# Setup's two transposes side by side, one more step between decay and outputs of the state space, and the row of its inverse norms put off by two units

## The chip, the core and the metric

The kernel runs on one core of one Trainium2 chip. A core has five engines with a queue each: TensorE (PE) for matrix products, VectorE (DVE), ScalarE (ACT), GpSimd (POOL), and SyncE (SP), which here only starts transfers. Each engine works through its own queue in order; an instruction that waits for another engine holds up what is queued behind it. The metric is the time of one execution in microseconds (us). Before the change it is 1207.95, the median of three runs (1207.37 to 1208.33).

## What is computed

Two layers over 256 tokens with 1024 features. Each layer adds to a residual `h` a gated feed-forward part, a mixer, and another feed-forward part. The mixer has a state-space branch of 16 heads in 2 groups, and an attention branch in which each token sees the 64 keys that an index score picks.

```python
for i in range(DEPTH):                                       # DEPTH = 2
    h = h + 0.5 * swiglu_ffn(rmsnorm(h, norm_ffn1[i]), w_ffn1_in[i], w_ffn1_out[i])
    u = rmsnorm(h, norm_mix[i]) @ w_mix_in[i]
    z, xbc, dt_raw, q, k, v, q_idx, k_idx, w_idx = jnp.split(u, SPLIT_POINTS, axis=-1)
    y_ssd = ssd_mixer(z, xbc, dt_raw, conv_w[i], conv_b[i], dt_bias[i], a_log[i], d_skip[i], ssd_norm[i])
    y_att = dsa_mixer(q, k, v, q_idx, k_idx, w_idx, positions)
    h = h + jnp.concatenate([y_ssd, y_att], axis=-1) @ w_mix_out[i]
    h = h + 0.5 * swiglu_ffn(rmsnorm(h, norm_ffn2[i]), w_ffn2_in[i], w_ffn2_out[i])
return rmsnorm(h, final_norm)
# the state space, per head: causal products with a decay exp(cs[l] - cs[s])
#   y = einsum('gls,gels,gsep->glep', C B^T, decay, x * dt) + x * d_skip
#   y = y * silu(z);  per group of 512 features: y * rsqrt(mean(y*y) + eps) * norm_g
```

## The kernel before

Every large product is made of three: an operand is split into a high and a low part, and PE forms high x high, high x low and low x high (`three`, L186 to L188; the mixer's channels L915 to L917). I call these main matmuls. They write 512 columns into one of the PSUM banks of the pools `mm` and `ac`, two banks each; short products and transposes use the pools `sd` and `tp`, two banks each. A bank can be written again only when it has been read.

Weights come through SP's queue in blocks of 128 x 2048 into a ring of three raw tiles. ACT casts each to its high part (`whi`, L128), DVE subtracts that from the raw tile (`wlo`, L129). These pairs are a ring of three as well: the cast of a new block waits until PE has done the last matmul of the block whose tiles it takes (`Stream.done`).

Side work is cut into generators, which `Flow.step` takes in turn, one step each time, between pieces of the main work; a `yield` ends a step. `Flow.defer(fn, units)` puts a function off by some units, and `Flow.unit` marks the end of one (in the output product 12 main matmuls). A scheduler then sets the final order on each engine from that program.

The mixer first projects in the order of `MIX_ORDER`, with the state space (`ssd`, added to the side work after channel 6) between q, k and v. For each group of 8 heads `ssd` fetches the running sums of the decay for 4 heads at a time into one of the two buffers of the ring `six()` (a transfer that POOL starts, L756), lets ACT form the decay (L758 to L763), lets DVE multiply it by C B^T (L764, L765), and lets PE form the outputs (L774, L778). `finish_y` then gates them, squares them, sums the squares on PE (`sums`, L805), takes the power -1/2 on POOL (L809), spreads the result over a bank by PE (`row`, L815), and scales and splits the outputs into `yT` (L824 to L827). The product with the output weights (`out_product`) goes through `yT` in pairs of 128-feature channels and calls `need` for each: 0 to 3 belong to the first group, 4 to 7 to the second, 8 to 15 to attention. Where one is missing, side work is stepped until it is there. Attention runs beside it: scores (L849), mask and maximum on DVE (L852, L856), exponentials on ACT (L859), division on DVE (L862, L863), transposes (L881 to L883) and outputs of each head (L871, L873), which ACT and DVE split (L876, L877).

Setup transposes two small tables on PE, gains (L377) and convolution weights (L379), into two places of one bank, and DVE copies each out (L378, L380).

Of the kernel before, what the change touches and what calls it, by code (L numbers as in the profile page):

```python
# [52 lines left out]
def hybrid_kernel(  # L53
# [6 lines left out]
    nc = tc.nc  # L60
# [288 lines left out]
    def setup():  # L349

        def later(*a, **k):
            tc.keep_in_program_order(nc.sync.dma_start(*a, **k))

        with tc.tile_pool(name="setup", bufs=1, reuse_waits="tile") as tmp:
            rows = tmp.tile([64, P], F32, name="rows")
            for i, v in enumerate((norm_ffn1, norm_mix, norm_ffn2, ssd_norm)):
                later(rows[16 * i:16 * i + 16, :], v.rearrange("l (k p) -> (l k) p", p=P))
            yield
            crows = tmp.tile([120, P], F32, name="crows")
            later(crows[0:96, :], conv_w.rearrange("l j (c p) -> (l j c) p", p=P))  # L360
            later(crows[96:120, :], conv_b.rearrange("l (c p) -> (l c) p", p=P))
            yield
            pos_i = tmp.tile([P, NT], I32, name="pos_i")
            later(pos_i, positions.rearrange("o (t p) -> p (o t)", p=P), allow_slow_non_contiguous=True)
            frq = tmp.tile([P, NF], F32, name="frq")
            later(frq, inv_freq.partition_broadcast(P))
            yield
            for i, v in enumerate((dt_bias, a_log, d_skip)):
                later(heads[:, i], v.partition_broadcast(P))
            yield  # L370
            for _ in range(3):
                yield
            for i in range(2):
                nc.gpsimd.tensor_copy(skips[64 * i:64 * i + 64],
                                      heads[64 * i:64 * i + 64, 2].rearrange("p l (c i) -> p l c i", i=2)[..., i])
            pg = bank(sd)
            nc.tensor.transpose(pg[:, 0:64], rows, ident[:64, :64])  # L377
            nc.vector.tensor_copy(gains, pg[:, 0:64])  # L378
            nc.tensor.transpose(pg[:, 128:248], crows, ident[:120, :120])  # L379
            nc.vector.tensor_copy(convs, pg[:, 128:248])  # L380
            yield
            pos = tmp.tile([P, NT], F32, name="pos")
            nc.vector.tensor_copy(pos, pos_i)
            ang = tmp.tile([P, NT, NF], F32, name="ang")
            turn = tmp.tile([P, NT, NF], F32, name="turn")
            for t in range(NT):
                nc.vector.tensor_scalar(ang[:, t], frq, pos[:, t:t + 1], None, op0=ALU.mult)
            yield
            RND = 12582912.0
            for period in (TWO_PI * 2048.0, TWO_PI):  # L390
                nc.vector.tensor_scalar(turn, ang, 1.0 / period, None, op0=ALU.mult)
                nc.vector.tensor_scalar(turn, turn, RND, None, op0=ALU.add)
                nc.vector.tensor_scalar(turn, turn, -RND, None, op0=ALU.add)
                for part in _pieces12(period, 3):
                    nc.vector.scalar_tensor_tensor(ang, turn, -part, ang, op0=ALU.mult, op1=ALU.add)
                yield
            PI_IN = 3.1415925
            nc.vector.tensor_scalar(ang, ang, PI_IN, -PI_IN, op0=ALU.min, op1=ALU.max)
            quarter = tmp.tile([P, NT, NF], F32, name="quarter")
            nc.vector.scalar_tensor_tensor(quarter, ang, -1.0, ang, op0=ALU.mult, op1=ALU.min)  # L400
            nc.vector.tensor_scalar(quarter, quarter, TWO_PI / 4, None, op0=ALU.add)
            yield
            cos_f = tmp.tile([P, NT, NF], F32, name="cos_f")
            sin_f = tmp.tile([P, NT, NF], F32, name="sin_f")
            nc.scalar.activation(cos_f, quarter, AF.Sin)
            nc.scalar.activation(sin_f, ang, AF.Sin)
            yield
            for name, c0 in (("att", 0), ("idx", 16)):
                cc, ss, n = ropes[name]
                for t in range(NT):  # L410
                    for half in range(2):
                        nc.gpsimd.tensor_copy(cc[:, t, half * n:(half + 1) * n], cos_f[:, t, c0:c0 + n])
                    nc.vector.tensor_scalar(ss[:, t, 0:n], sin_f[:, t, c0:c0 + n], -1.0, None, op0=ALU.mult)
                    nc.gpsimd.tensor_copy(ss[:, t, n:2 * n], sin_f[:, t, c0:c0 + n])
            yield
# [155 lines left out]
    def mixer(l, norm, after):  # L571
        with ExitStack() as mctx:
# [165 lines left out]
            def ssd():  # L738
                cb = ms.tile([P, G_SSD, 384], F32, name="cb")
                for g in range(G_SSD):  # L740
                    ps = bank(sd)
                    bm, cm = chan[8 + g], chan[10 + g]
                    nc.tensor.matmul(ps[:, 0:L], bm[:, 0:P], cm, start=True, stop=True)
                    nc.tensor.matmul(ps[:, L:L + P], bm[:, P:L], cm[:, P:L], start=True, stop=True)
                    nc.vector.tensor_mul(cb[:, g, 0:L], ps[:, 0:L], mask01)
                    nc.vector.tensor_mul(cb[:, g, L:384], ps[:, L:384], triu)
                yield
                for g in range(G_SSD):
                    ms4 = []
                    for h0 in (0, 4):  # L750
                        m = six()
                        m0 = m[:, 0:1024].rearrange("p (h c) -> p h c", h=4)
                        m1 = m[:, 1024:1536].rearrange("p (h c) -> p h c", h=4)
                        ms4.append((m0, m1))
                        hh = 8 * g + h0
                        nc.gpsimd.dma_start(m0, csum[hh:hh + 4, :].partition_broadcast(P))  # L756
                        for h in range(4):
                            nc.scalar.activation(m1[:, h], m0[:, h, P:], AF.Relu, scale=-1.0,  # L758
                                                 bias=cs[:, 1, hh + h:hh + h + 1])
                            nc.scalar.activation(m0[:, h], m0[:, h], AF.Relu, scale=-1.0,  # L760
                                                 bias=cs[:, 0, hh + h:hh + h + 1])
                        nc.scalar.activation(m0, m0, AF.Exp, scale=-1.0)
                        nc.scalar.activation(m1, m1, AF.Exp, scale=-1.0)  # L763
                        nc.vector.tensor_mul(m0, m0, bc(cb[:, g, 0:L], [P, 4, L], 1))  # L764
                        nc.vector.tensor_mul(m1, m1, bc(cb[:, g, L:384], [P, 4, P], 1))  # L765
                        yield
                    half = xs[:, :, 512 * g:512 * g + 512]
                    pss = [bank(ac) for _ in range(2)]
                    for h in range(0, 8, 2):
                        o = pss[h // 4][:, h % 4 * P:h % 4 * P + L]  # L770
                        m0, m1 = ms4[h // 4]
                        for j in range(2):
                            tc.keep_in_program_order(
                                nc.tensor.matmul(o[64 * j:64 * j + 64], half[:, 0, (h + j) * 64:(h + j + 1) * 64],  # L774
                                                 m0[:, (h + j) % 4], start=True, stop=False))
                        for j in range(2):
                            tc.keep_in_program_order(
                                nc.tensor.matmul(o[64 * j:64 * j + 64, P:], half[:, 1, (h + j) * 64:(h + j + 1) * 64],  # L778
                                                 m1[:, (h + j) % 4], start=False, stop=True))
                    finish_y(g, half, pss)  # L780
                    yield

            def finish_y(g, half, pss):
# [18 lines left out]
                def sums():  # L802
                    ps = bank(sd)
                    for t in range(NT):
                        nc.tensor.matmul(ps[:, t:t + 1], sz[:, 4 * g, t * P:(t + 1) * P], ones[:, 0:1],  # L805
                                         start=True, stop=True)
                    m, rg = (small.tile([P, NT], F32, name=n) for n in ("ms_y", "r_y"))
                    nc.vector.tensor_scalar(m, ps[:, 0:NT], 2.0 / D_SSD, EPS, op0=ALU.mult, op1=ALU.add)
                    nc.gpsimd.tensor_tensor(rg, m, mhalf.to_broadcast([P, NT]), ALU.pow)  # L809
                    flow.defer(lambda: row(rg))  # L810

                def row(rg):
                    rT = bank(sd)[:, :L]
# [223 lines left out]
```

## Time and profile before

| what | value |
|---|---|
| median of 3 runs | 1207.95 us |
| profiled execution | 1208.47 us |
| its span, first to last instruction | 1206.8 us |
| PE busy | 1192.7 us, 99% |
| DVE busy | 738.4 us, 61% |
| ACT busy | 634.1 us, 53% |
| POOL busy | 101.9 us, 8% |
| moved by DMA | 214.26 MB, 178 GB/s over the span |

The profiled execution is the one that all times of the trace come from; 1.67 us of it lie outside the span. The share of PE says that the kernel is as long as PE's work and waits; the list of PE's waits is short. The other engines' shares are averages over parts with different work. In the rows a tile's name stands without its number, and "x4" behind a row are several like instructions in one.

### The profile page before, as it was taken

What the parts mean: (1) busy time and instruction counts of PE and PEld (TensorE: products, weight loads), DVE (VectorE), ACT (ScalarE), POOL (GpSimd) and SP (SyncE); (2) the same over time, 40 slices, a digit from 0 to 9 for tenths busy, and PEclk for the clock granted to TensorE, in tenths of its full rate; (3) what the DMA queues carried; (4) which work ended last, traced back from release to release, by engine and by line L of the source; (5) the groups of instructions that cost most, each with busy time, mean ns of one, the idle gap of its engine ahead of it and who ended that gap; (6) DMA issues with size and microseconds to landing.
All of it is one profiled execution on the core that took longest, in us unless ns stands there. A gap on an engine that the chain in (4) does not pass through costs nothing.

```text
span 1206.8 us, 15519 instructions
## 1 busy us (share of the span) xinstructions
PE 1192.7 (99%) x6125; PEld 1002.6 (83%) x6125; DVE 738.4 (61%) x948; ACT 634.1 (53%) x847; POOL 101.9 (8%) x206
## 2 busy tenths in 40 slices
PE   9999999999999999999999999999999999999997
PEld 7788888998777888888888888899987788888886
DVE  5645545796797555544465554467868965554544
ACT  7544435658775544443354444366478555444432
POOL 1200000502410000000000000014133000000000
PEclk9999999999999999999999999999999999999999
DMA  9565555654534465555655645466455435556550
GB/s 291 171 205 184 186 175 165 210 175 158 192 140 145 135 210 187 164 207 188 196 161 188 201 163 198 163 205 196 145 191 192 140 122 174 191 164 204 183 200 36
DMA packets 152909, 214.26 MB, mean 178 GB/s; under 512 B 8068, under 2 KB 123012, under 8 KB 152836
## 3 DMA queue, kind: packets, MB, share of 16 engines
q1 hardware_dynamic: 151108, 207.99, 52.6%
q0 software_dynamic: 1280, 4.23, 1.0%
q8 instruction: 48, 0.79, 0.3%
q10 hardware_dynamic: 448, 1.05, 0.2%
q14 instruction: 25, 0.20, 0.1%
HBM read 212.17 MB, written 1.08 MB: 177 GB/s over the span
## 4 chain that ended last, share of the span: by engine, by line
PE 89%; ACT 5%; DMA 2%; DVE 1%; issue 1%; POOL 1%; SPq 0%; POOLq 0%; ACTq 0%
PE mm L187 14%; PE mm L188 13%; PE mm L186 13%; PE ac L188 11%; PE ac L187 11%; PE ac L186 11%; PE mm L915 2%; PE ac L915 2%; PE mm L917 2%; PE ac L916 2%; PE ac L917 2%; PE mm L916 2%; PE tp L541 2%; ACT whi L128 1%; PE sd L849 1%
## 5 line engine op out<-in xcount | busy, mean ns | idle before, releaser
L129 DVE TENSOR_TENSOR wlo<-raw,whi 128x2048 fp32r<-128x2048 f32 (+3 forms) x208 | 451.7, 2176 | 325.2 <-ACT whi L128 324.4
L128 ACT CAST whi<-raw 128x2048 fp32r<-128x2048 f32 (+3 forms) x208 | 376.8, 1818 | 285.5 <-PE ac L188 193.0
L186 PE MATMUL mm<-whi,tT 128*128 128x512 f32 (+1 forms) x640 | 255.2, 399 | 0.0
L187 PE MATMUL mm<-wlo,tT 128*128 128x512 f32 (+1 forms) x640 | 247.9, 387 | 0.9 <-DVE wlo L129 0.9
L188 PE MATMUL mm<-whi,tT 128*128 128x512 f32 (+1 forms) x640 | 248.1, 388 | 0.0
L186 PE MATMUL ac<-whi,tT 128*128 128x512 f32 (+1 forms) x448 | 176.5, 394 | 0.0
L188 PE MATMUL ac<-whi,tT 128*128 128x512 f32 (+1 forms) x448 | 173.3, 387 | 0.0
L187 PE MATMUL ac<-wlo,tT 128*128 128x512 f32 (+1 forms) x448 | 173.1, 386 | 0.0
L187 PEld LDWEIGHTS mm<-wlo,tT 128*128 128x128 f32 x640 | 120.6, 188 | 24.1 <-DVE wlo L129 1.4
L188 PEld LDWEIGHTS mm<-whi,tT 128*128 128x128 f32 x640 | 120.3, 188 | 24.4
L186 PEld LDWEIGHTS mm<-whi,tT 128*128 128x128 f32 x640 | 120.6, 188 | 23.5 <-issue 1.3
L188 PEld LDWEIGHTS ac<-whi,tT 128*128 128x128 f32 x448 | 84.3, 188 | 16.4
L187 PEld LDWEIGHTS ac<-wlo,tT 128*128 128x128 f32 x448 | 84.6, 189 | 15.4 <-DVE wlo L129 0.4
L186 PEld LDWEIGHTS ac<-whi,tT 128*128 128x128 f32 x448 | 84.3, 188 | 14.7
L186 PE MATMUL ac<-whi,hT_hi 128*128 128x512 f32 x176 | 69.3, 394 | 0.0
L186 PE MATMUL mm<-whi,hT_hi 128*128 128x512 f32 x176 | 69.0, 392 | 0.0
L188 PE MATMUL ac<-whi,hT_lo 128*128 128x512 f32 x176 | 68.6, 390 | 0.0
L188 PE MATMUL mm<-whi,hT_lo 128*128 128x512 f32 x176 | 68.6, 390 | 0.0
L187 PE MATMUL mm<-wlo,hT_hi 128*128 128x512 f32 x176 | 68.5, 389 | 0.0
L187 PE MATMUL ac<-wlo,hT_hi 128*128 128x512 f32 x176 | 68.5, 389 | 0.0
L450 POOL TENSOR_TENSOR r_x<-ms_x,mhalf 128x1 f32<-128x1 f32 x12 | 6.6, 547 | 670.7 <-DVE ms_x L448 663.2
L563 ACT ACTIVATE s1k<-mm,r_x 128x256 f32<-128x256 f32 x44 | 20.7, 471 | 69.7 <-PE mm L188 69.7
(230 smaller groups left out, 1604.6 us busy)
## 6 DMA issues: line engine op xcount, KB each, us to landing
raw<-in_w_ffn_in_dram SPq DMA_DIRECT2D x172, 512.0 KB, 4.9
raw<-in_w_ffn_out_dram SPq DMA_DIRECT2D x44, 1024.0 KB, 4.9
raw<-in_w_mix_in_dram SPq DMA_DIRECT2D x44, 1024.0 KB, 5.2
raw<-in_w_mix_out_dram SPq DMA_DIRECT2D x16, 1024.0 KB, 4.8
s<-csum POOLq DMA_DIRECT2D x8, 512.0 KB, 4.1
raw<-in_w_mix_in_dram SPq DMA_DIRECT2D x4, 600.0 KB, 3.9
raw<-in_w_mix_in_dram SPq DMA_DIRECT2D x4, 568.0 KB, 3.9
raw<-in_w_ffn_in_dram SPq DMA_DIRECT2D x8, 256.0 KB, 6.0
```

Source lines behind the costliest of these rows:

```text
L128: pin(nc.scalar.copy(hi[:, o], raw[:, o]))
L129: pin(nc.vector.tensor_sub(lo[:, o], raw[:, o], hi[:, o].bitcast(F32)))
L186: nc.tensor.matmul(ps, xh, whi, start=first, stop=False)
L187: nc.tensor.matmul(ps, xh, wlo, start=False, stop=False)
L188: nc.tensor.matmul(ps, xl, whi, start=False, stop=last)
L450: nc.gpsimd.tensor_tensor(r, m, mhalf, ALU.pow)
L541: nc.tensor.transpose(ps[:, f * L + t * P:f * L + (t + 1) * P], hs[:, t, f * P:(f + 1) * P], ident)
L563: nc.scalar.activation(sg, ps[:, 0:256], AF.Silu, scale=norm.r[t])
L849: nc.tensor.matmul(ps[:, j * nk:(j + 1) * nk], qT[:, hg + h0 + j, t * P:(t + 1) * P], kT[:, hg + h0 + j, 0:nk], start=True, stop=True)
L915: nc.tensor.matmul(ps, hi[:, o:o + P], xh, start=(k == 0), stop=False)
L916: nc.tensor.matmul(ps, hi[:, o:o + P], xl, start=False, stop=False)
L917: nc.tensor.matmul(ps, lo[:, o:o + P], xh, start=False, stop=(k == KD - 1))
```

## The change

Three edits. In setup both transposes are issued before the first copy. In `ssd` one more `yield` stands between the last decay of a group and its outputs, so another generator or a piece of main work can come between. The function `row` is put off by two units and not by one. Behind the added line every line number is one higher: L774 is L775, L815 is L816, L877 is L878, L882 is L883.

```diff
--- before.py
+++ after.py
@@ -375,8 +375,8 @@
                                       heads[64 * i:64 * i + 64, 2].rearrange("p l (c i) -> p l c i", i=2)[..., i])
             pg = bank(sd)
             nc.tensor.transpose(pg[:, 0:64], rows, ident[:64, :64])
+            nc.tensor.transpose(pg[:, 128:248], crows, ident[:120, :120])
             nc.vector.tensor_copy(gains, pg[:, 0:64])
-            nc.tensor.transpose(pg[:, 128:248], crows, ident[:120, :120])
             nc.vector.tensor_copy(convs, pg[:, 128:248])
             yield
             pos = tmp.tile([P, NT], F32, name="pos")
@@ -764,6 +764,7 @@
                         nc.vector.tensor_mul(m0, m0, bc(cb[:, g, 0:L], [P, 4, L], 1))
                         nc.vector.tensor_mul(m1, m1, bc(cb[:, g, L:384], [P, 4, P], 1))
                         yield
+                    yield
                     half = xs[:, :, 512 * g:512 * g + 512]
                     pss = [bank(ac) for _ in range(2)]
                     for h in range(0, 8, 2):
@@ -807,7 +808,7 @@
                     m, rg = (small.tile([P, NT], F32, name=n) for n in ("ms_y", "r_y"))
                     nc.vector.tensor_scalar(m, ps[:, 0:NT], 2.0 / D_SSD, EPS, op0=ALU.mult, op1=ALU.add)
                     nc.gpsimd.tensor_tensor(rg, m, mhalf.to_broadcast([P, NT]), ALU.pow)
-                    flow.defer(lambda: row(rg))
+                    flow.defer(lambda: row(rg), 2)
 
                 def row(rg):
                     rT = bank(sd)[:, :L]
```

On PE in setup, as a difference (`rows`, `crows`: the two tables; `sd`: the bank):

```order
 L377 MATMUL sd<-ident,rows 128x64
-L186 MATMUL ac<-whi,tT 128x512
-L187 MATMUL ac<-wlo,tT 128x512
-L188 MATMUL ac<-whi,tT 128x512
-L186 MATMUL ac<-whi,tT 128x512
-L187 MATMUL ac<-wlo,tT 128x512
-L188 MATMUL ac<-whi,tT 128x512
-L186 MATMUL ac<-whi,tT 128x512
-L379 MATMUL sd<-ident,crows 128x120
+L378 MATMUL sd<-ident,crows 128x120
```

The transpose of `crows`, L379 before and L378 now, stands right behind L377, and the seven main matmuls come behind both.

On ACT in layer 0, around the outputs of the first group, before (`s6_3047`: the buffer of the second group's first four heads, filled by the transfer that DMASW4 stands for; `whi`: a cast of weights):

```order
L895 COPY s8_1649<-tp_3031 128x4x128 [waits PE_49]
L758 ACTIVATE s6_3047<-s6_3047,cs_1644 128x128 [waits DMASW4_49]
L758 ACTIVATE s6_3047<-s6_3047,cs_1644 128x128
L760 ACTIVATE s6_3047<-s6_3047,cs_1644 128x256 [waits Activation_49] x2
L758 ACTIVATE s6_3047<-s6_3047,cs_1644 128x128 x2
L760 ACTIVATE s6_3047<-s6_3047,cs_1644 128x256 [waits Activation_49]
L796 ACTIVATE s8_1647<-s8_1648 128x512 [waits DVE_49]
```

And now (`s6_3104` is that buffer):

```order
L896 COPY s8_1649<-tp_3013 128x4x128 [waits PE_49]
L945 ACTIVATE s2_3037<-mm_2980,r_x_1580 128x512 [waits Pool_49]
L758 ACTIVATE s6_3104<-s6_3104,cs_1644 128x128 [waits DMASW4_49,PE_49]
L797 ACTIVATE s8_1647<-s8_1648 128x512 [waits DVE_49]
L760 ACTIVATE s6_3104<-s6_3104,cs_1644 128x256 [waits Activation_49]
L758 ACTIVATE s6_3104<-s6_3104,cs_1644 128x128
L128 CAST whi_3060<-raw_2922 128x2048 [waits DMAHW4_49,PE_49]
```

The first reader of this buffer, L758, now waits for PE as well as for the transfer, behind it stands the cast `whi_3060`, and an eviction of a main bank, L945, stands ahead of it instead of behind.

On PE in the output product of layer 0, the place where a block of weights is freed between two attention heads, before (`whi_3357`: the block, `sd_3485` and `sd_3504`: outputs of two heads):

```order
L186 MATMUL ac_3398<-whi_3357,tT_3264 128x512
L187 MATMUL ac_3398<-wlo_3358,tT_3264 128x512
L871 MATMUL sd_3485<-s2_3471,s8_1651 128x256 [waits DVE_49,PE_49]
L873 MATMUL sd_3485<-s2_3471,s8_1651 128x128
L871 MATMUL sd_3504<-s2_3496,s8_1651 128x256 [waits DVE_49]
L873 MATMUL sd_3504<-s2_3496,s8_1651 128x128
L188 MATMUL ac_3398<-whi_3357,tT_3265 128x512
L186 MATMUL ac_3399<-whi_3357,tT_3264 128x512
L849 MATMUL sd_3521<-s8_1649,s8_1650 128x128 [waits DVE_49]
```

The same two heads now (`whi_3297` the block, whose last matmul is the first row; `sd_3512` the row of the second group's norms; each pair L872 and L874 one head):

```order
L188 MATMUL ac_3383<-whi_3297,tT_3355 128x512
L872 MATMUL sd_3474<-s2_3466,s8_1651 128x256 [waits DVE_49]
L874 MATMUL sd_3474<-s2_3466,s8_1651 128x128
L872 MATMUL sd_3493<-s2_3485,s8_1651 128x256 [waits DVE_49,Activation_49]
L874 MATMUL sd_3493<-s2_3485,s8_1651 128x128
L816 MATMUL sd_3512<-ident_99,r_y_3433 128x128 [waits DVE_49,Pool_49]
L816 MATMUL sd_3512<-ident_99,r_y_3433 128x128
L850 MATMUL sd_3539<-s8_1649,s8_1650 128x128 [waits DVE_49]
L850 MATMUL sd_3539<-s8_1649,s8_1650 128x128 x3
```

The second group's row, which stood some fifty rows further up, now follows the two heads, takes the bank of the first of them, and waits for DVE as well as for POOL. Between the block's last matmul and the row stand these two heads alone.

On DVE at the same place, before:

```order
L129 TENSOR_TENSOR wlo_3482<-raw_3355,whi_3481 128x2048 [waits DMAHW2_49,Activation_49]
L877 TENSOR_TENSOR tT_3445<-sd_3441,tT_3444 128x256 [waits Activation_49]
L877 TENSOR_TENSOR tT_3464<-sd_3460,tT_3463 128x256 [waits PE_49,Activation_49]
L877 TENSOR_TENSOR tT_3489<-sd_3485,tT_3488 128x256 [waits Activation_49]
L877 TENSOR_TENSOR tT_3508<-sd_3504,tT_3507 128x256 [waits Activation_49]
L852 SCALAR_TENSOR_TENSOR s6_3517<-sd_3521,bias0_2792 128x512 [waits PE_49]
```

And now (`tT_3478`: the low part of the head whose bank the row takes):

```order
L889 COPY s2_3466<-tp_3462 128x384 [waits PE_49,Pool_49]
L878 TENSOR_TENSOR tT_3459<-sd_3455,tT_3458 128x256 [waits Activation_49]
L129 TENSOR_TENSOR wlo_3509<-raw_3330,whi_3508 128x2048 [waits DMAHW3_49,Activation_49]
L878 TENSOR_TENSOR tT_3478<-sd_3474,tT_3477 128x256 [waits Activation_49]
L878 TENSOR_TENSOR tT_3497<-sd_3493,tT_3496 128x256 [waits Activation_49]
L825 SCALAR_TENSOR_TENSOR s8_1648<-s8_1648,gains_117,sd_3512 128x256 [waits PE_49]
```

The weight subtraction L129 now stands between the readers of the heads, in front of `tT_3478`; before, it stood in front of all four.

## Rows read from the trace of the kernel before

**Rows 1.** The page: span and busy time of each engine.

```profile
span 1206.8 us, 15519 instructions
PE 1192.7 (99%) x6125; PEld 1002.6 (83%) x6125; DVE 738.4 (61%) x948; ACT 634.1 (53%) x847; POOL 101.9 (8%) x206
```

**Rows 2.** What TensorE waited for: us in total, times, longest us.

```profile
PE sd L815 <- POOL r_y L809: 1.8, 2, 0.9
PE ac L774 <- DVE s L764: 1.0, 2, 0.5
PE tp L894 <- POOL s L427: 0.8, 2, 0.4
```

**Rows 3.** Timeline at setup's transposes: start us, duration us, engine, line, [idle before <-releaser].

```profile
45.46 0.39 PE L186 MATMUL ac<-whi,tT 128*128 128x512 f32 x1
46.71 0.22 DVE L378 COPY gains<-sd 128x64 f32<-128x64 f32 x1
46.98 0.32 PE L379 MATMUL sd<-ident,crows 120*128 120x120 f32 x1 [1.14 <-DVE gains L378]
```

**Rows 4.** Timeline, layer 0, first step's decay and the two transfers around it.

```profile
315.36 0.54 POOL L756 DMA_DIRECT2D s<-csum  x1 [4.63 <-PE ac L778]
320.37 1.23 DVE L764 TENSOR_TENSOR s<-s,cb 128x1024 f32<-128x1024 f32 x1 [0.26 <-ACT s L762]
322.23 0.72 ACT L758 ACTIVATE s<-s,cs 128x128 f32<-128x128 f32 x2
323.11 0.50 PE L186 MATMUL mm<-whi,tT 128*128 128x512 f32 x1
328.69 0.60 PE L894 MATMUL tp<-ident,s 128*128 128x128 f32 x4
329.05 0.48 PE L186 MATMUL mm<-whi,tT 128*128 128x512 f32 x1
331.71 0.58 ACT L895 COPY s<-tp 128x512 f32<-128x512 f32 x1
```

**Rows 5.** Instructions of tile csum: the time of its transfers to landing.

```profile
DMA to landing us min/median/max: 1.6/4.0/4.7
```

**Rows 6.** Timeline, layer 0, attention beside the first rows of the norm.

```profile
357.64 0.69 DVE L852 SCALAR_TENSOR_TENSOR s<-sd,bias 128x512 f32<-128x512 f32 x1 [0.16 <-PE sd L849]
358.97 2.28 DVE L129 TENSOR_TENSOR wlo<-raw,whi 128x2048 fp32r<-128x2048 f32 x1
363.79 0.48 PE L186 MATMUL ac<-whi,tT 128*128 128x512 f32 x1
364.11 0.39 PE L187 MATMUL ac<-wlo,tT 128*128 128x512 f32 x1
```

**Rows 7.** Timeline, layer 0, where a weight block is freed between attention heads.

```profile
369.83 0.49 PE L188 MATMUL ac<-whi,tT 128*128 128x512 f32 x1
370.39 1.91 ACT L128 CAST whi<-raw 128x2048 fp32r<-128x2048 f32 x1 [1.90 <-PE ac L188]
372.33 2.29 DVE L129 TENSOR_TENSOR wlo<-raw,whi 128x2048 fp32r<-128x2048 f32 x1 [2.75 <-ACT whi L128]
374.55 0.74 DVE L877 TENSOR_TENSOR tT<-sd,tT 128x256 fp32r<-128x256 f32 x2
375.11 0.67 PE L871 MATMUL sd<-s,s 128*128 128x256 f32 x2
376.41 0.48 PE L188 MATMUL ac<-whi,tT 128*128 128x512 f32 x1
```

**Rows 8.** Timeline of TensorE, first main matmuls of the program.

```profile
7.51 0.78 PE L186 MATMUL mm<-whi,tT 128*128 128x512 f32 x1
10.20 0.39 PE L186 MATMUL mm<-whi,tT 128*128 128x512 f32 x1
```

**Rows 9.** Stretches after TensorE's last matmul: busy time by engine, granted clock.

```profile
1200.00:1204.00 4.00, 0.02 (x1) 0.00 (x0) 2.16 (x5) 1.63 (x4) 0.54 (x1) 1.00 0.05 19
1204.00:1206.80 2.80, 0.00 (x0) 0.00 (x0) 0.00 (x0) 0.00 (x0) 0.00 (x0) 0.65 0.43 160
```

## The prediction, made before the changed kernel was run

> **What bounds the kernel now.** I read the page first: TensorE (PE) is busy 1192.7 of 1206.8 us, VectorE (DVE) 61%, ScalarE (ACT) 53% [rows 1]. So the end moves only by what PE does more or less, or by what it waits for; time saved on another engine counts only where PE was waiting for it. The second view is the list of PE's waits. The reader is to see how little there is to win: the three waits at which the edits point are 1.8 us (two rows of inverse norms, for GpSimd's power), 1.0 us (two outputs, for DVE's product with the decay), 0.8 us (two transposes behind GpSimd's rotation) [rows 2] and 1.14 us (setup's second transpose, for the copy of the first) [rows 3]. The third view is the timeline around those places, where I looked at what else becomes late if an instruction stands somewhere else. The fourth is the order of both kernels, which says behind what each instruction is queued; times for that order I take from the trace alone.
>
> One main matmul costs 0.23 us: 24 of them stand between 323.11 and 328.69 [rows 4]. The first after another kind of instruction costs 0.09 more: 363.79 to 364.11 is 0.32 [rows 6].
>
> **Setup.** The copy of the gains waits on DVE and starts at 46.71, and PE stands before the second transpose until 46.98, while its matmul of 45.46 should have been followed after 0.23 [rows 3]. Now both transposes stand together; DVE's copies come behind both and nobody on PE waits for them soon. Gain: 46.98 - 45.46 - 0.23 = 1.29, and one return to main matmuls fewer, 0.09: **-1.4 us**, once. Bounds: 0, if the second transpose has to wait for its rows, and -1.4; I take the latter, since the wait in the trace names the copy on DVE and no transfer.
>
> **The row of inverse norms one unit later.** A unit of the output product is 12 main matmuls, 2.8 us by the spacing above. The wait that it is to cover is 0.9 us per row [rows 2]. So this wait goes: -0.9 per layer for the one row where it showed (the list has 1.8 in 2, one in each layer). The waits for the rotation, 0.4 per layer, go too, since those transposes now come after more main matmuls: -0.4. Order shows 26 instead of 29 returns to main matmuls in a layer's mixer: -0.3. Together **-1.6 per layer**, at best; at least 0.
>
> **The extra step.** It issues nothing. The outputs of heads 0 to 7 come 24 main matmuls later, at once for both halves. It does not save PE's wait there: the product that the second half needs ends on DVE at 320.37 + 1.23 = 321.60 [rows 4]. PE stood before it for 0.5 [rows 2], so it was there at 321.1; now the first half's outputs stand right in front, with two returns fewer, so at 320.9, and it waits 0.7. The main matmul behind it starts near 323.1 in both. What it does move is the buffer. In the kernel before, GpSimd issues the next transfer at 315.36, when the first half's outputs have ended [rows 4]. Now these end at about 320.9; with an allowance of 0.3 it is issued at 321.2; landing 4.0 later in the median and 4.7 at most [rows 5], so 325.2 to 325.9. ACT works through its queue in order, and the activation that reads this buffer stands ahead of two weight casts and of an eviction that frees a bank of PE's. Before, ACT went from this activation at 322.23 to the same point behind the two casts at 331.71, 9.5 us [rows 4], with almost the same instructions; add 0.6 for the eviction (as long as the copy of 331.71). From 325.4, a little above the median, this gives 335.5. PE asks for the bank after two stretches of 24 main matmuls and two groups of transposes: 323.11 + 2 x (328.69 - 323.11) + 2 x (329.05 - 328.69) = 335.0 [rows 4]. New wait **+0.5 per layer**; bounds 0 (an early landing) and 1.2 (a landing 0.7 later).
>
> **What both edits do to the output product.** The first row of norms now comes just before attention's first transposes, and the second between attention heads. Two places suffer.
>
> The first transposes wait for a softmax division on DVE. In front of it stand the addition of the mask and a maximum, a weight subtraction, one scaling by the new row, and the division. From 357.64 to the subtraction's end, 358.97 + 2.28, this took 3.6 us in the trace, and two such short instructions took 358.97 - 357.64 = 1.33 [rows 6]. With 0.56 from a matmul's start to the engine that waits for it (369.83 to 370.39 [rows 7]) it is 5.5. PE has meanwhile 12 main matmuls, 2.8, and five to six products of heads and row, 0.22 each (six take 376.41 - 375.11 = 1.30 [rows 7]): about 4.2. Wait +1.3. Then the low half of the first product channel is queued behind one more weight subtraction: 0.66 + 2.2 + 0.66 = 3.5 against 2.1 of PE's work, less what of it ran beside the former wait: +0.8. Together **+2.1 per layer**, bounds 1.0 and 2.5.
>
> The second row needs a bank that a head's output still holds. That head is read by DVE behind a weight subtraction, which needs ACT's cast, which needs the block that PE's last main matmul of this part frees. All of that chain is in the trace, in another place: matmul at 369.83, cast at 370.39, subtraction at 372.33, the next instruction at 374.55, which takes 0.4 [rows 7]. So the row can start 374.55 + 0.4 - 369.83 = 5.1 after that matmul, and 0.1 for the way back. PE has only that matmul, 0.23, and two heads, 1.30 [rows 7], since the next channels of the output product wait for this row: 5.2 - 1.5 = **+3.7 per layer**. In the kernel before, the row came earlier and main matmuls stood behind the freed block: PE was at the next head only at 375.11, 5.28 after 369.83 [rows 7], and did not wait. Bounds: 1.8, if the cast is done when PE gets there (1.9 less), and 4.3, if a copy is first on ACT (0.3) and the first scaled channel is late as well (0.3).
>
> A rule of the Trainium skill speaks against any of this: TensorE: Matmul & The Clock Gate, Part 1, says that a PE left idle falls back to 1.2 GHz, so a long wait would cost twice. What it would cost is the rival "clock" below.
>
> **Sum.** Per layer 0.5 + 2.1 + 3.7 - 1.6 = +4.7; two layers +9.4; setup -1.4; together +8.0. The profiled execution took 1208.47 (1.67 us around the span of 1206.8 [rows 1]), so 1216.5. It lies 0.52 above the median of the runs, 1207.95; against the median I predict **1216.0**. With the low ends (0 + 1.0 + 1.8 - 1.6 = 1.2 per layer) it is 1208.0 + 2.4 - 1.4 = 1209.0; with the high ones (1.2 + 2.5 + 4.3 - 1.6 = 6.4) 1208.0 + 12.8 - 1.4 = 1219.4.
>
> **Rivals.**
> All waits go and none comes. The price is 1.4 + 2 x 1.6 = 4.6, so 1203.4. For it: all three waits are real, and 99% busy says that PE mostly has work. Against it: between that last main matmul and the second row PE needs 3.7 us more work than the order gives it, 16 main matmuls. From there on it decides; with them it would be this case.
>
> Chains partly covered. The casts run earlier than in the place that I took them from, and only the low ends come true: 1209.0, no change. For it: ACT is busy half of the time, so it often starts at once. Against it: the cast cannot start before the block is free, whatever ACT does.
>
> Nothing in place of the extra step. If the scheduler keeps the second half where it was, the buffer is not late and only the rows count: 2 x (2.1 + 3.7 - 1.6) - 1.4 = +7.0, 1215.0. This stands within the forecast.
>
> Clock. PE idles near 4 us before the second row. At the program's start its matmuls came at half pace: six of them from 7.51 to 10.20 [rows 8], 2.69 us for 6 x 0.23 = 1.38, the lower of its two levels (1.2 of 2.4 GHz). If the level fell after each long wait and came back as late as there, 1.3 each, 2.6 in all: 1218.6. Against it: in the four microseconds behind its last matmul the granted clock was still 1.00, and only the stretch from 1204 has 0.65 [rows 9]. [...]
>
> **Chances.** A measurement of this kernel tells some 0.2%, 2.4 us, from no change. Forecast with its own range 1212 to 1219.4, the third rival included: 0.62. Partly covered, 1205.6 to 1212: 0.20, of which 0.12 within 0.2%, 0.07 slower and 0.01 faster. All waits gone: 0.08. Clock: 0.10, all slower. Of the case without waits 0.07 is faster and 0.01 no change. So faster 0.08, within 0.2% 0.13, slower 0.79. The range 1208.5 to 1220 holds the forecast, most of the clock case and the upper half of the partly covered.
>
> **What would show it.** Lines behind the added one are one higher there. In the list of PE's waits: the row (L816 now) behind DVE L878, twice, about 3.7 each, as the largest; attention's transposes (L882) behind DVE L864, twice, above 1; a main matmul behind ACT L945, near 0.5; and L379, the row behind POOL and L894 gone. On ACT 2 to 3 us idle before L758 behind GpSimd's transfer. Layer 0's last part should begin some 3.3 us later than in the kernel before (4.7 less setup's 1.4). I am wrong if the row's wait is under 1.8, if DVE's subtraction there is finished before the heads, or if PE has main matmuls between the heads and the row.

## Result, and the profile after

The changed kernel takes 1216.51 us in the median of four runs (1215.10 to 1218.84), against 1207.66 of the kernel before in four runs: a ratio of 1.0075, 95% interval 1.0057 to 1.0092. It is slower, by 8.9 us. The profiled execution took 1216.30, 7.83 more than that of the kernel before. The page, span and busy time:

```profile
span 1214.6 us, 15537 instructions
PE 1194.7 (98%) x6125; PEld 1004.3 (83%) x6125; DVE 739.2 (61%) x948; ACT 635.6 (52%) x847; POOL 98.1 (8%) x206
```

PE's work is the same within 2 us [rows 1]; its span is 7.8 longer. Where this is lost is read from one instruction that both kernels have in the same place, the addition to the residual (DVE L528). Before, the last one ahead of layer 0's mixer and the first after each mixer began at

```profile
198.01 0.69 DVE L528 SCALAR_TENSOR_TENSOR h_res<-ac,h_res 128x512 f32<-128x512 f32 x1 [0.47 <-PE ac L188]
...
410.50 0.68 DVE L528 SCALAR_TENSOR_TENSOR h_res<-mm,h_res 128x512 f32<-128x512 f32 x1
...
1006.13 0.68 DVE L528 SCALAR_TENSOR_TENSOR h_res<-mm,h_res 128x512 f32<-128x512 f32 x1
```

and now:

```profile
196.54 0.69 DVE L528 SCALAR_TENSOR_TENSOR h_res<-ac,h_res 128x512 f32<-128x512 f32 x1 [0.46 <-PE ac L188]
...
413.81 0.68 DVE L528 SCALAR_TENSOR_TENSOR h_res<-mm,h_res 128x512 f32<-128x512 f32 x1
...
1013.99 0.68 DVE L528 SCALAR_TENSOR_TENSOR h_res<-mm,h_res 128x512 f32<-128x512 f32 x1
```

The columns are start, duration, engine, line. So the kernel was 198.01 - 196.54 = 1.47 ahead when the first mixer began and 413.81 - 410.50 = 3.31 behind at its end; at the end of the second it was 7.86 behind. Layer 0's mixer cost 4.8 us and layer 1's, entered at 3.3 behind, 4.5. Outside the mixers nothing was won or lost behind setup. Layer 1's figure also holds a wait for weights (L187 behind DVE L129, at 897.89 before), 0.9 in the profile before and 0.2 in this one; in the profiles of the other kernels below it is between nothing and 1.1, so it belongs to the execution and not to the change. Of the 1.47, 0.24 was there before setup's transposes (L377 at 43.52, against 43.76 before), from the first loads.

The list of PE's waits (total, times, longest) answers to [rows 2]:

```profile
PE sd L816 <- DVE tT L878: 6.3, 2, 3.2
PE tp L882 <- DVE s L864: 2.6, 2, 1.3
PE ac L775 <- DVE s L764: 1.4, 2, 0.7
PE mm L188 <- DVE tT L828: 0.6, 2, 0.3
PE sd L872 <- DVE s L889: 0.3, 2, 0.2
PE mm L186 <- ACT s L945: 0.2, 1, 0.2
```

The mixers' waits for GpSimd are gone (one of 1.1 at the program's start is the same in both), and so is the one for the copy of the gains. In their place the first two lines stand, 8.9 us in all. That this equals the loss is chance: the waits that went were 3.7 [rows 2] [rows 3], and something is lost that no line of this list has. Setup on PE, which answers to [rows 3], has no wait any more:

```profile
43.52 0.27 PE L377 MATMUL sd<-ident,rows 64*128 64x64 f32 x1
43.72 0.32 PE L378 MATMUL sd<-ident,crows 120*128 120x120 f32 x1
43.80 0.48 PE L186 MATMUL ac<-whi,tT 128*128 128x512 f32 x1
```

For the largest wait, the chain of work between 373 and 379 says what it was made of (start, duration, engine, instruction):

```profile
373.63 0.24 ACT s L887
374.01 1.91 ACT whi L128
375.94 2.29 DVE wlo L129
378.24 0.35 DVE tT L878
378.72 0.68 PE sd L816 x4
```

ACT copies a transposed head, then casts the freed weights for 1.91; DVE subtracts them for 2.29, then reads the head whose bank the row needs; then PE may go on. PE had nothing between 375.6 and 378.72. This is the chain that [rows 7] showed in another place.

What follows on PE is not in any list of waits:

```profile
378.72 0.68 PE L816 MATMUL sd<-ident,r_y 128*128 128x128 f32 x4 [3.15 <-DVE tT L878]
379.24 1.84 PE L850 MATMUL sd<-s,s 128*128 128x128 f32 x8
380.73 0.77 PE L186 MATMUL mm<-whi,tT 128*128 128x512 f32 x1
381.30 0.63 PE L187 MATMUL mm<-wlo,tT 128*128 128x512 f32 x1
381.73 0.63 PE L186 MATMUL mm<-whi,tT 128*128 128x512 f32 x1
```

The main matmuls behind the row are 0.43 apart (381.30 to 381.73), not 0.23. The granted clock of the same place (start and end, length, PE busy, clock, share and rate of DMA):

```profile
376.00:378.00 2.00, 0.00 (x0) 1.00 0.00 0
378.00:380.00 2.00, 1.28 (x8) 0.83 0.28 51
380.00:382.00 2.00, 2.00 (x9) 0.50 0.95 385
382.00:384.00 2.00, 2.00 (x9) 0.82 0.22 88
```

PE stands idle from 376 to 378 at full clock; the clock falls only in the stretch where it works again, is 0.50 in the next, the lower of its two levels, and comes back in the last.

### The profile page after: what moved, and what is told of

It reads as the page before. It is cut to its first block, busy times and chain, and to the rows that moved or that the text cites. A ratio compares the mean times of both kernels' runs of the same rounds, so it can differ in the third digit from the quotient of the medians.

```text
span 1214.6 us, 15537 instructions
## 1 busy us (share of the span) xinstructions
PE 1194.7 (98%) x6125; PEld 1004.3 (83%) x6125; DVE 739.2 (61%) x948; ACT 635.6 (52%) x847; POOL 98.1 (8%) x206
## 4 chain that ended last, share of the span: by engine, by line
PE 89%; ACT 3%; DVE 3%; DMA 2%; issue 1%; SPq 0%; POOLq 0%; POOL 0%; ACTq 0%
PE mm L188 14%; PE mm L186 14%; PE mm L187 14%; PE ac L188 11%; PE ac L187 11%; PE ac L186 11%; DVE wlo L129 2%; PE tp L541 2%; DMA raw<-in_w_ffn_in_dram 2%; PE mm L916 2%; PE ac L916 2%; PE mm L918 1%; PE ac L918 1%; PE ac L917 1%; PE mm L917 1%; ACT whi L128 1%
## 5 line engine op out<-in xcount | busy, mean ns | idle before, releaser
L129 DVE TENSOR_TENSOR wlo<-raw,whi 128x2048 fp32r<-128x2048 f32 (+3 forms) x208 | 451.5, 2175 | 324.6 <-ACT whi L128 324.1
L187 PE MATMUL mm<-wlo,tT 128*128 128x512 f32 (+1 forms) x640 | 248.8, 389 | 0.4 <-DVE wlo L129 0.2
L187 PE MATMUL ac<-wlo,tT 128*128 128x512 f32 (+1 forms) x448 | 172.4, 385 | 0.2 <-DVE wlo L129 0.2
L187 PEld LDWEIGHTS mm<-wlo,tT 128*128 128x128 f32 x640 | 121.2, 189 | 22.8 <-DVE wlo L129 1.6
L187 PEld LDWEIGHTS ac<-wlo,tT 128*128 128x128 f32 x448 | 84.4, 188 | 16.1 <-DVE wlo L129 1.0
L187 PE MATMUL mm<-wlo,hT_hi 128*128 128x512 f32 x176 | 68.5, 389 | 0.0
L187 PE MATMUL ac<-wlo,hT_hi 128*128 128x512 f32 x176 | 68.5, 389 | 0.0
```

Source lines behind the costliest of these rows:

```text
L129: pin(nc.vector.tensor_sub(lo[:, o], raw[:, o], hi[:, o].bitcast(F32)))
L187: nc.tensor.matmul(ps, xh, wlo, start=False, stop=False)
```

## Experiments

Each kernel was timed beside the kernel before, whose median was 1207.61 beside the first four and 1207.42 beside the other three. In parentheses stand the lowest and highest run behind a time, and the 95% interval behind a ratio to the kernel before. The lines in their profiles are one higher behind an added line.

**One edit alone, and two together.** The first three kernels are the three pieces of the diff shown above, one in each; the fourth has setup's piece and the later row.

> Setup's transposes side by side alone. My theory (each edit's effect adds up by waits): PE's wait behind the copy of the gains goes and nothing else moves, -1.2 to -1.4 us, about 1206.4. Rival (setup's time is given back, since the weights of the first part set the pace there): no change within 0.3 us.

Setup alone: 1206.67 against 1207.61, ratio 0.9991 (0.9983 to 1.0000). PE's wait behind the copy of the gains is gone. That is 0.9 less, a little under what was expected, and the interval reaches from 2 us to none, so the time alone does not rule out the rival. The trace does: from the first transpose (44.32) to the last L528 ahead of layer 0's mixer (197.35) it has 153.03 us, the kernel before 154.25 (43.76 to 198.01). So 1.2 is won there and not given back.

> The extra step alone, the row put off by one unit as before. Theory A (the loss comes from the extra step: it makes the outputs late, and with them the second row, so that main matmuls run out while ACT and DVE split the next weights; the later row is not needed for it): +3 to +4.5 us a layer, 1214 to 1217, with a wait of about 3 us on DVE between attention heads in each layer. Theory B (only both edits together bring the row behind the heads): at most +1.5 us a layer, under 1211.

The extra step alone: 1213.00 (1209.94 to 1216.67), ratio 1.0045 (1.0031 to 1.0059). The two waits that stand out in it are the same chain, parted in two, since the row here comes before the last heads and not behind them:

```profile
PE sd L872 <- DVE tT L878: 3.7, 2, 1.9
PE sd L816 <- DVE tT L878: 1.8, 2, 0.9
```

So the extra step alone brings a loss, and theory B is out by the median, though this lies 1 us below the range that A gave, and one run of six is under B's 1211. The runs lie 6.7 apart, and they order themselves by the mean granted clock: 1209.94 at 0.998, 1211.28 at 0.997, 1211.60 at 0.996, 1214.41 and 1214.47 at 0.994, 1216.67 at 0.993. The first of them, at a clock that the kernel before has too (0.998 and 0.999), is 2.3 slower than that kernel; of the 5.4 at the median the larger part goes with the clock. In the profiled one, the slowest of these:

```profile
374.00:376.00 2.00, 0.33 (x3) 0.87 0.00 0
376.00:378.00 2.00, 1.82 (x5) 0.50 0.58 92
378.00:380.00 2.00, 2.00 (x6) 0.50 1.02 420
380.00:382.00 2.00, 2.00 (x7) 0.50 0.03 12
```

PE waits 0.9, does the row until 374.3, and waits 1.85 until 376.18. The clock falls within this second wait, and is at the lower level for 6 us and more.

> The row two units later alone, without the extra step. Theory A: the wait for GpSimd's power goes and the row's place still has main matmuls around it, -0.5 to -1 us a layer, 1206 to 1207. Theory B: a part of the loss is here already, +1 us a layer or more, 1210 or above.

The later row alone: 1205.24, ratio 0.9981 (0.9972 to 0.9989), faster by 2.4. The wait for GpSimd's power, 1.8 us before [rows 2], is gone, and no new one of note has come; in the mixers the other two of [rows 2] are left, 1.0 and 0.8, and 0.3 for weights in layer 1. It is a little more than the range of theory A. This edit by itself does what it was made for.

> Setup's transposes side by side and the row two units later, without the extra step: the sum of both alone, by theory A 1204.5 to 1206 and the fastest of all; by theory B 1208 or above.

Both of these: 1204.29 (1203.76 to 1204.79), ratio 0.9973 (0.9962 to 0.9984). The gains add up, 0.9 + 2.4 = 3.3, and the time is a little under the range of theory A. It is the fastest kernel of this study, 12.2 us under the changed one. All three edits together do not add up: 0.9 less, 5.4 more and 2.4 less would make 2.1 more, and the changed kernel has 8.9 more. With the extra step, the later row takes nothing away, since no wait for GpSimd's power is left in the list of the extra step alone. It moves the row behind the heads, where no main matmul follows until the row is done, and it brings the wait of attention's first transposes, 2.6, which neither edit has alone.

**The chain itself.** In the next kernel the block of weights is freed where it was, but its cast and subtraction are issued behind the second row's scaling. The last piece of the diff holds ACT's cast of the scaled outputs at its place in the program.

```diff
@@ out_product
             if need:
                 need(j + 1)
+                if j == 4:
+                    was, strict[0] = strict[0], True
+                    stream.done()
+                    strict[0] = was
...
-                if t == 1:
+                if t == 1 and not (need and j == 2):
                     stream.done()
@@ scale
-                            nc.scalar.copy(hi, y[:, b, i])
+                            cast = nc.scalar.copy(hi, y[:, b, i])
+                            if g:
+                                tc.keep_in_program_order(cast)
```

> The changed kernel, with the one weight block that is freed between the attention heads cast and subtracted behind the second row's scaling instead of ahead of it; TensorE's order is the same. Theory A (TensorE stands idle because this cast and subtraction, 1.9 and 2.2 us, are queued ahead of the reader of the bank that the row needs; the clock falls only as a result): the wait of the row shrinks from 3.2 to about 0.4 us a layer, the matmuls behind it come 0.23 apart and not 0.43, 8 us less in all, about 1208. Rival (the row's own chain, its power on GpSimd or the heads, is late anyway): the wait stays above 2 us, 1214 to 1217.

1208.99 (1207.91 to 1209.70), ratio 1.0013 (1.0004 to 1.0022): 7.5 us less than the changed kernel. PE's order of work is the same up to the row and some 10 us beyond it; from 386.5 on it differs a little, so the order did not stay wholly unchanged as expected. In the list of waits L820 is the row, L884 the head's reader, L888 the first transposes of attention, L951 the eviction of a main bank:

```profile
PE tp L888 <- DVE s L870: 2.6, 2, 1.3
PE mm L186 <- ACT s L951: 1.2, 2, 1.1
PE sd L820 <- DVE tT L884: 0.7, 2, 0.4
```

The row waits 0.36 in place of 3.15, and the matmuls behind it keep their pace:

```profile
375.93 0.68 PE L820 MATMUL sd<-ident,r_y 128*128 128x128 f32 x4 [0.36 <-DVE tT L884]
377.62 0.50 PE L186 MATMUL mm<-whi,tT 128*128 128x512 f32 x1
377.96 0.40 PE L187 MATMUL mm<-wlo,tT 128*128 128x512 f32 x1
378.20 0.39 PE L186 MATMUL mm<-whi,tT 128*128 128x512 f32 x1
```

So the cast and the subtraction ahead of the head's reader made the wait, and the slow stretch came from the wait. What stays is 1.6 us above the kernel before, with the wait of the first transposes, which this edit leaves, 2.6, and one for a bank.

**The clock.** This kernel fills the wait with matmuls that nobody reads.

```diff
@@ row
                 def row(rg):
+                    if g:
+                        fill = bank(tp)
+                        xh = yT[0][0]
+                        for _ in range(24):
+                            nc.tensor.matmul(fill[:, :L], xh[:, :P], xh, start=True, stop=True)
                     rT = bank(sd)[:, :L]
```

> The changed kernel, with 24 matmuls of 256 columns that nobody reads (0.12 us each, 2.9 us in all) on TensorE where it waits for the second row; nothing else moves. Theory A (behind the wait TensorE's clock is at the lower level because it had been idle): the row comes when it came, the matmuls behind it are 0.23 apart, about 1.5 us a layer less, 1213 to 1214, and the runs lie closer together. Rival (the slow matmuls behind the wait come from something else, weights that arrive or a busy DVE): still 0.43 apart and 1216 to 1217, or more by what the filling costs.

1213.41 (1212.48 to 1213.77), ratio 1.0045 (1.0033 to 1.0058): 3.1 us less than the changed kernel, and no run of one within the runs of the other. On PE (L818 the filling, L821 the row):

```profile
375.70 3.11 PE L818 MATMUL tp<-tT 128*128 128x256 f32 x24
379.10 0.68 PE L821 MATMUL sd<-ident,r_y 128*128 128x128 f32 x4 [0.29 <-DVE tT L883]
380.79 0.50 PE L186 MATMUL mm<-whi,tT 128*128 128x512 f32 x1
381.13 0.40 PE L187 MATMUL mm<-wlo,tT 128*128 128x512 f32 x1
381.37 0.40 PE L186 MATMUL mm<-whi,tT 128*128 128x512 f32 x1
```

The row comes as late as before, 5.37 after the matmul that frees the block (373.73 to 379.10; in the changed kernel 373.35 to 378.72), but the main matmuls behind it are 0.34 and 0.24 apart. The granted clock there is full, although DVE is as busy as in the slow stretch of the changed kernel (all of the 2 us in both) and nearly as much arrives by DMA (313 against 385 GB/s):

```profile
380.00:382.00 2.00, 1.88 (x12) 1.00 0.82 313
```

So the rival is out. The lower clock was paid for idling, 1.55 us a layer by the medians. The wider spread of the changed kernel's runs (3.7 us in four runs; here 1.3 in five) fits with it. So does the kernel with the late cast: 2 x 2.79 for the row's wait and 3.1 for the clock, less 1.0 for the longer wait for a bank (1.2 against 0.2), make 7.7, and it took 7.5 less.

**The bank.** The rows take a bank of the transposes' pool.

```diff
@@ row
-                    rT = bank(sd)[:, :L]
+                    rT = bank(tp)[:, :L]
```

> The changed kernel, with the rows of the inverse norms in a bank of the transposes' pool instead of the heads' pool. Theory A (the bank is only where the wait shows; the weight subtraction stands ahead of what TensorE needs in any case): the row's wait goes, a wait of 2 to 3 us behind DVE shows at a head or a main matmul instead, 1214 to 1218. Rival (the row waits only because of its bank): 3 us a layer less and the clock's 1.5, 1207 to 1209.

1211.57 (1210.41 to 1215.61), ratio 1.0036 (1.0024 to 1.0048): 4.9 us less, between the two theories, so neither was right in size. The scheduler gave this kernel another order, with the row in two halves between the heads, so it is not the bank alone that changed. The waits:

```profile
PE sd L872 <- DVE s L889: 2.4, 4, 0.7
PE tp L816 <- ACT s L887: 1.3, 2, 0.7
PE tp L882 <- DVE s L864: 0.9, 2, 0.5
PE sd L872 <- ACT s L887: 0.4, 2, 0.2
```

For heads and row these lines add up to 4.1, where 6.3 + 0.3 stood before, the first transposes wait 0.9 in place of 2.6, and no single one of these waits is over 0.7. The mean granted clock of the profiled execution is 0.999; the slowest run, 1215.61, has 0.997. The row did not get ahead of the weights' subtraction: in layer 0 this ends on DVE at 374.57, the row's first half begins at 374.58, released by a copy on ACT, and the next head then waits 0.7 for a copy that DVE makes behind the subtraction. This is the part of theory A that held. What the bank is worth in an unchanged order this run does not show.

## Why the prediction came out

The time, 1216.0, was met within 0.5 us, and the mixers' +4.7 a layer by 4.8 and 4.5. The parts were met less well, and two misses cancelled: that the sum came so near is luck.

- **Setup, -1.4.** About 1.2 by the trace (1.47 less the 0.24 that came earlier), 0.9 by the timing of it alone. Right in kind, a little too large.
- **The three waits, -1.6 a layer.** The mixers' waits for GpSimd are gone from the list as forecast. Alone, the later row brought 1.2 a layer; the 0.4 for the rotation stays with it and goes only with the extra step.
- **The extra step saves nothing at the decay.** Right: the wait behind L764 went from 0.5 to 0.7 and stands at the same product.
- **The late buffer, +0.5.** ACT's reader began at 323.63, after 2.14 of idling for the transfer, and the bank came free at the end of L945:

```profile
323.63 0.40 ACT L758 ACTIVATE s<-s,cs 128x128 f32<-128x128 f32 x1 [2.14 <-DMA s<-csum]
333.02 0.67 ACT L945 ACTIVATE s<-mm,r_x 128x512 f32<-128x512 f32 x1
```

PE waited 0.2 for it in layer 1 and not at all in layer 0. The mechanism is there, the size was nearer to the lower bound, since this transfer, issued at 319.78, was read 3.85 later, not 4.2; in layer 1 it was 4.1. In the kernel with the late cast, whose order is the same here, layer 1's transfer was read 5.0 after its issue (915.15 to 920.14), and PE's wait for the bank is 1.1, so the upper bound of 1.2 was no idle one.
- **The first transposes, +2.1.** 1.31 a layer, plus 0.29 for the low half of the first channel: 1.6. DVE's queue stood as forecast, mask, maximum, weight subtraction, division:

```profile
352.74 0.68 DVE L853 SCALAR_TENSOR_TENSOR s<-sd,bias 128x512 f32<-128x512 f32 x1
354.27 2.28 DVE L129 TENSOR_TENSOR wlo<-raw,whi 128x2048 fp32r<-128x2048 f32 x1
356.92 0.68 DVE L864 TENSOR_TENSOR s<-s,rinv 128x512 f32<-128x512 f32 x1
```

The first part was met (1.3), but with both of its sides 0.45 too short: from the scores (L850) at 351.79 to the transposes at 357.75 it took 5.96, not 5.5, since DVE began the mask only behind other work, and PE's work in between was 4.65, not 4.2. The second part was taken 0.5 too large. The cause of this wait was not tested by a run of its own.
- **The second row, +3.7.** 3.15 a layer, from the chain as forecast. The chain was right: from the matmul at 373.35 to the row at 378.72 it took 5.37, forecast 5.2. PE's own time beside it was too short by 0.7: it had work until 375.57 (378.72 less 3.15), 2.2 after that matmul and not 1.5, since the next head began only 0.64 later, 0.16 of it a wait, and the heads took a little longer.
- **The clock, a rival with a chance of 0.10.** This step of my reasoning failed. I held against it that the clock was still 1.00 in the four microseconds behind PE's last matmul [rows 9]. That stretch told less than I thought: behind a wait of 3.15, shorter than those four, the changed kernel shows the lower level, though only after PE works again. The rival was priced at 1.3 a layer; the filled wait says 1.55. TensorE: Matmul & The Clock Gate, Part 1, of the Trainium skill says that an idle PE falls to 1.2 GHz; here the runs agree, with 0.50 granted in 380 to 382, behind the wait of 3.15 in the changed kernel.

The waits were thus forecast at 6.3 a layer and came to 3.15 (the row) + 1.6 (the first transposes and the low half) + 0.2 (a head, L872) + 0.1 (the buffer, mean of both layers) = about 5.0. They were taken 1.3 too long, and the clock, 1.55, was left out. With the 1.6 that was won this makes 5.0 a layer, where 4.8 and 4.5 were measured. The range would have held either case; the clock was no rival to the forecast but a consequence of it, and should have been a term of the sum behind the row's wait. Behind the first transposes' wait of 1.3 the profile shows no such fall.

The rival in which all waits go and none comes was wrong for this change, but without the extra step the kernel comes near the time worked out for it: 1204.29, against 1203.4, with the wait for the rotation (0.8 in all) still there. The point from which it decides was the one named, whether PE has main matmuls between the freed block and the row: in that kernel they begin up to 366.60, and layer 0's second row follows at 366.83 without a wait.

## What to carry to other kernels

A busy engine waits where the next instruction that it needs stands behind a long instruction for later work in another engine's queue: look there, at what each newly placed instruction comes behind, before counting what the move saves. Edits that each remove a wait may not be added up where they change the same order; time them apart. And where TensorE will wait some microseconds, as here 3.15, count the slower matmuls behind the wait too, or give it something to do.

## What was not expected of the hardware

In layer 0 of the changed kernel the granted clock did not fall while PE idled but in the 2 us after it had begun again (0.83 in 378 to 380, 0.50 in 380 to 382). It is not always so: with the extra step alone it fell inside a wait (0.87 in 374 to 376, where PE stood from 374.3 to 376.18), and at the end of the kernel before it fell with PE idle [rows 9]. There the fall came inside the second of two waits, 0.9 and 1.85, with a short row between them; with single waits up to 0.7 in that place and heads between them the profiled execution of the last kernel stayed at 0.999, though its slowest run has 0.997. It does not cost the same in each execution: with the extra step alone the runs went from 1209.94 to 1216.67, in the order of their granted clock.
